# A hybrid decoder block on one core: the first norm's row blocks put in another order

## The chip, the cores and the metric

The kernel runs on one core of a Trainium2 chip. The time is device microseconds of one execution, as the median of several runs. A core has a matrix engine (TensorE, PE in the profile, with PEld for its weight loads), a vector engine (VectorE, DVE), an activation engine (ScalarE, ACT), a general engine (GpSimd, POOL) and a queue engine (SyncE, SP). Each works through its own fixed queue of instructions in order; semaphores tie the queues together. TensorE writes to eight banks of PSUM; everything else lies in SBUF, 128 partitions wide. Transfers from memory are issued by SP, ACT or POOL and run on 16 DMA engines.

## The reference

`x` is 512 rows (tokens) of 2048 columns. What the change touches is the start:

```python
def rmsnorm(x, g):
    xf = x.astype(jnp.float32)
    y = xf * lax.rsqrt(jnp.mean(xf * xf, axis=-1, keepdims=True) + EPS)
    return (y * g.astype(jnp.float32)).astype(x.dtype)
...
        h = rmsnorm(x, g_mix[l])
        z = jnp.einsum('bsd,dc->bsc', h, w_in[l])
        cb, cc, cv, q, k, v, f_logit, gate_c, gate_a = jnp.split(z, SPLIT_POINTS, axis=-1)
```

Behind it come a gated short convolution and eight attention heads with a forget bias, an output projection onto the residual, a second norm with a squared-ReLU MLP of 8192 columns, and a last norm. All of it is in float32.

## The kernel before

**Numbers.** A float32 product is made of three fp32r products: each operand is split into a high part `hi` (ScalarE copies it to fp32r, line 100) and a low part `lo` (VectorE subtracts, line 101); then hi·hi, lo·hi and hi·lo are added up in PSUM. `split` (line 99) does this for weights (tiles `th`, `tl`, two buffers each) and for activations.

**Strassen.** The wide projections use Strassen's scheme in Winograd's form on halves: two halves of the tokens (256 each) by two halves of the 2048 inputs (the even and the odd blocks of 128). `Quarters` (line 378) makes the activation side: `H[i, par]` is the normalised, turned `x` for token half i and input parity par. From it come seven tiles, each with a high and a low part: A11 and A12 (the first token half), A22, and the four sums S1 to S4, which `Quarters.sums` (line 423) makes in place in H with four VectorE steps and then splits in the order S4, S2, S3, S1. The tile of S1 lies over H[0,0] and H[1,0], those of S4 and S2 over the loaded rows of `x`.

**Groups.** A `Group` (line 173) is a set of columns of a weight matrix. Its `head` (line 227) loads two quarters of the weights, and makes the products with A11 (bank "a") and A12 (bank "b"); ScalarE copies a (`snap`), VectorE adds b (`plus`), and the result is stored. Its `tail2` (line 282) loads four quarters and makes the products with S1, S3, S2, S4 and A22, in this order, with VectorE subtracting weights before each. The first groups are gV0 (half of the attention values; `mm_rows`, line 150, with tokens as the output's partitions) and four K/Q groups (`mm_cols`, line 128). Their five heads run first (lines 504 to 506), then the four sums are made, then the five tails. So the heads need the first token half alone, and everything from the first tail on needs all 512 tokens.

**The first norm.** `x` is loaded in four row blocks of 128 tokens (lines 439 to 443) on SP's queue, block 0 in quarters, the others in halves; the small parameter rows are loaded by ACT's queue, turned by TensorE (`pv`, line 453) and copied to `cols`, which holds the gains. For each block ScalarE squares four quarters and adds them up (line 376), VectorE adds the four sums (line 370), POOL raises the result to the power -1/2 (line 372), and VectorE makes a diagonal matrix `dg` of the factors (line 406). TensorE multiplies each 128x128 piece of the rows by `dg` (line 410), which turns and scales it at once; four such pieces fill a bank, 6 or 7 by turns, and VectorE evicts the bank in two steps, one for each parity, with the gain (line 415). Blocks 0 and 1 are written before the squares of 2 and 3; blocks 2 and 3 before the first head.

**What sets the order.** The program is traced as written, and a planner orders each engine's instructions before the run: of those it takes to be ready it issues the earliest in the program. The result is a fixed queue for every engine. Loads wait for a free slot of four (`x0` to `x3`), splits for one of two buffers.

## Time and profile before

| what | value |
|---|---|
| median of three runs | 2464.81 us (2460.54 to 2464.90) |
| the profiled execution's own time | 2467.16 us |
| its span, first to last instruction | 2464.4 us |
| mean granted TensorE clock | 0.998 |
| PE busy | 2435.7 us (99%) |
| DVE busy | 1922.2 us (78%) |
| ACT busy | 1148.4 us (47%) |
| POOL busy | 180.1 us (7%) |
| moved by DMA | 462.98 MB, 188 GB/s |

A row of the timeline has the start in us from the first instruction, the length in us, the engine, the line of the kernel, the operation, the tiles written and read, the shapes, how many instructions were merged, and in square brackets the idle time of the engine before it with what ended it. A row of the chain of waits has the start, the length, the engine, the tile and the line. A row of a group ends with busy us, mean ns of one, and idle time before. Matmuls overlap, so two starts tell more of their price than a length does. An engine that is full on average may be far from full in a stage, and the other way round.

### The profile page before, as it was taken

Reading aid. Unit: us, or ns where it says so; the run is one execution under the profiler, and the core shown is the slowest. Engines: PE = TensorE matmul, PEld = TensorE weight load, DVE = VectorE, ACT = ScalarE, POOL = GpSimd, SP = SyncE. Lnnn points to the kernel's source line nnn. Section 1 sums busy time; section 2 is a strip of 40 time slices with the busy share of each in tenths; the row PEclk is TensorE's granted clock in tenths of the full one; section 3 lists DMA queues with packets and bytes.
Section 4 is the critical chain, followed back from the end, with each engine's and each line's share of the span. In section 5 each row is a group of like instructions: output and inputs, shape, how many; then the busy total and the mean of one; then the engine's idle time right before and its main releaser. Section 6 shows DMA issues by size and latency. Waiting matters only on the chain.

```text
span 2464.4 us, 39238 instructions
## 1 busy us (share of the span) xinstructions
PE 2435.7 (99%) x16910; PEld 2251.2 (91%) x16910; DVE 1922.2 (78%) x1595; ACT 1148.4 (47%) x1144; POOL 180.1 (7%) x280
## 2 busy tenths in 40 slices
PE   7999999999999999999999999999999999999998
PEld 7999999999999988888899999999998888888886
DVE  7977777788777744526688898888987888889898
ACT  6443434334544532225555666656665333333334
POOL 0100000001000000000000000000011001100000
PEclk9999999999999999999999999999999999999999
DMA  7564544456544554335645646656488576655662
GB/s 245 178 186 150 157 133 144 146 175 210 164 125 140 181 175 154 124 128 196 200 164 199 232 176 210 214 194 234 167 298 296 169 250 225 235 194 183 238 229 95
DMA packets 272033, 462.98 MB, mean 188 GB/s; under 512 B 10268, under 2 KB 172180, under 8 KB 271732
## 3 DMA queue, kind: packets, MB, share of 16 engines
q1 hardware_dynamic: 235136, 303.13, 38.7%
q0 software_dynamic: 35856, 156.25, 16.9%
q8 instruction: 132, 2.16, 0.4%
q10 hardware_dynamic: 868, 1.10, 0.1%
q14 instruction: 41, 0.34, 0.0%
HBM read 368.16 MB, written 92.27 MB: 187 GB/s over the span
## 4 chain that ended last, share of the span: by engine, by line
PE 92%; DVE 5%; DMA 1%; issue 1%; ACT 1%; POOL 0%; SPq 0%; DVEq 0%; POOLq 0%; ACTq 0%
PE a L144 6%; PE a L146 6%; PE a L148 6%; PE d L148 5%; PE d L144 5%; PE d L146 5%; PE a L162 4%; PE a L164 4%; PE a L161 4%; PE c L146 4%; PE c L144 4%; PE c L148 4%; PE d L161 2%; PE d L162 2%; PE d L164 2%; PE b L144 2%
## 5 line engine op out<-in xcount | busy, mean ns | idle before, releaser
L100 ACT ACTIVATE th<-x 128x2048 fp32r<-128x2048 f32 (+1 forms) x252 | 483.1, 1917 | 497.3 <-DVE x L104 161.7
L101 DVE TENSOR_TENSOR tl<-x,th 128x2048 fp32r<-128x2048 f32 (+1 forms) x252 | 575.4, 2287 | 169.3 <-ACT th L100 154.6
L104 DVE TENSOR_TENSOR x<-x,x 128x2048 f32<-128x2048 f32 (+1 forms) x144 | 329.4, 2288 | 11.4 <-DMA x<-in_w_in_dram 5.5
L100 ACT ACTIVATE th<-y 128x2048 fp32r<-128x2048 f32 x81 | 155.5, 1921 | 225.4 <-PE a L162 138.5
L101 DVE TENSOR_TENSOR tl<-raw,th 128x2048 fp32r<-128x2048 f32 x40 | 91.7, 2292 | 150.8 <-ACT th L100 150.3
L162 PE MATMUL a<-th,us 128*128 128x512 f32 x512 | 199.2, 389 | 0.0
L161 PE MATMUL a<-th,us 128*128 128x512 f32 x512 | 199.2, 389 | 0.0
L101 DVE TENSOR_TENSOR tl<-y,th 128x2048 fp32r<-128x2048 f32 x81 | 185.1, 2287 | 16.9 <-ACT th L100 16.7
L144 PE MATMUL a<-ST,th 128*128 128x256 f32 x752 | 174.8, 278 | 1.3 <-ACT th L100 1.3
L146 PE MATMUL a<-ST,th 128*128 128x256 f32 x752 | 174.4, 277 | 0.0
L100 ACT ACTIVATE th<-raw 128x2048 fp32r<-128x2048 f32 x40 | 76.7, 1918 | 176.4 <-PE pt L344 62.6
L144 PEld LDWEIGHTS a<-ST,th 128*128 128x128 f32 x752 | 141.4, 188 | 1.7 <-ACT th L100 1.7
L146 PEld LDWEIGHTS a<-ST,th 128*128 128x128 f32 x752 | 141.4, 188 | 0.0
L164 PE MATMUL a<-tl,us 128*128 128x512 f32 x512 | 136.9, 389 | 0.6 <-DVE tl L101 0.6
L144 PE MATMUL c<-S,th 128*128 128x256 f32 x576 | 134.7, 278 | 0.0
L146 PE MATMUL c<-S,th 128*128 128x256 f32 x576 | 134.5, 278 | 0.0
L144 PE MATMUL d<-ST,th 128*128 128x256 f32 x512 | 118.9, 277 | 0.0
L146 PE MATMUL d<-ST,th 128*128 128x256 f32 x512 | 118.9, 277 | 0.0
L100 ACT ACTIVATE th<-t 128x2048 fp32r<-128x2048 f32 x31 | 59.5, 1919 | 125.1 <-DVE t L104 72.7
L164 PEld LDWEIGHTS a<-tl,us 128*128 128x128 f32 x512 | 95.9, 188 | 21.1 <-DVE tl L101 1.0
L161 PEld LDWEIGHTS a<-th,us 128*128 128x128 f32 x512 | 96.1, 188 | 20.0
L162 PEld LDWEIGHTS a<-th,us 128*128 128x128 f32 x512 | 96.1, 188 | 19.9
(296 smaller groups left out, 6381.0 us busy)
## 6 DMA issues: line engine op xcount, KB each, us to landing
x<-in_w_in_dram SPq DMA_DIRECT2D x86, 1024.0 KB, 5.8
x<-in_w_ff_dram SPq DMA_DIRECT2D x64, 1024.0 KB, 7.4
y<-in_w_ff_dram SPq DMA_DIRECT2D x64, 1024.0 KB, 8.0
us<-s_d POOLq DMA_DIRECT2D x48, 1024.0 KB, 9.5
s_d<-rh POOLq DMA_DIRECT2D x32, 896.0 KB, 5.5
s_d<-r POOLq DMA_DIRECT2D x32, 896.0 KB, 5.7
raw<-in_w_mix_out_dram SPq DMA_DIRECT2D x24, 1024.0 KB, 5.1
g_d<-o POOLq DMA_DIRECT2D x32, 256.0 KB, 3.0
```

What stands on the lines that cost most here:

```text
L100: nc.scalar.activation(out=hi, in_=src, func=AF.Copy)
L101: nc.vector.tensor_tensor(out=lo, in0=src, in1=hi.bitcast(F32), op=ALU.subtract)
L104: nc.vector.tensor_tensor(out=out, in0=a, in1=b, op=ALU.subtract)
L144: nc.tensor.matmul(o, hi[:, q, js], Sh, start=first and q == 0 and j == 0, stop=False, skip_group_check=True)
L146: nc.tensor.matmul(o, hi[:, q, js], Sl, start=False, stop=False, skip_group_check=True)
L148: nc.tensor.matmul(o, lo[:, q, js], Sh, start=False, stop=q == nq - 1, skip_group_check=True)
L161: nc.tensor.matmul(o, Sh, hi[:, q, :], start=begin and q == 0, stop=False, skip_group_check=True)
L162: nc.tensor.matmul(o, Sl, hi[:, q, :], start=False, stop=False, skip_group_check=True)
L164: nc.tensor.matmul(o, Sh, lo[:, q, :], start=False, stop=q == nq - 1, skip_group_check=True)
```

## The change

Five things in the opening are different.

- Loads: block 0 and block 1 of `x` are issued by SP and ACT by turns; the parameter rows go to POOL's queue; the weights of gV0's head are issued before the rows of blocks 2 and 3, which come as one transfer each.
- 28 turns of the identity into an unused bank are put in front of the first block's turn.
- Block 0 is turned into four banks (0, 1, 2, 5) and block 1 into 6, 7, 0, 1, with the eviction on VectorE written as a function of its own (`gained`). Block 1 and the later ones have one square over 2048 columns; POOL adds epsilon and takes the power, and ScalarE makes the diagonal.
- gV0's head (`first_rows`) runs its product with A11 for the first 128 tokens, then for the second; block 1's eviction and the splits of A12 stand between.
- Blocks 2 and 3 are squared after gV0's head (the square of block 2 writes the cell that gV0's copy reads as its scale, 1.0), turned together in pieces of two, eight pieces after the head of the first K/Q group and eight after that of the second, and evicted by ScalarE with the gain as its scale (`gained_both`). A22 is then split in one.

```diff
--- before.py
+++ after.py
@@ -399,26 +399,35 @@
         def put(self, n, src, ts=slice(0, HS)):
             split(src[:, :, ts], self.ST[n][:, 0, :, ts], self.ST[n][:, 1, :, ts])
 
-        def block(self, xt, part, t):
-            r = rstd_of(part)
+        def turn(self, ts, cs, dgs, banks):
+
+            n = S // (P * len(ts))
+            out = []
+            for c, i in zip(range(cs.start, cs.stop, n), banks):
+                pt = bank(i, "ptr").rearrange("p (k s) -> p k s", k=n)
+                for k in range(n):
+                    for e, t in enumerate(ts):
+                        nc.tensor.matmul(pt[:, k, e * P:(e + 1) * P], xin[t][:, (c + k) * P:(c + k + 1) * P], dgs[t],
+                                         start=True, stop=True)
+                out.append((c, pt))
+            return out
+
+        def gained(self, t, turned):
+
             i, ts = t // 2, slice(t % 2 * P, (t % 2 + 1) * P)
-            dg = const.tile([P, P], F32, tag="dg", name="dg", bufs=2)
-            nc.vector.tensor_scalar(out=dg, in0=ident, scalar1=r, scalar2=None, op0=ALU.mult)
-            for c in range(4):
-                pt = bank(6 + c % 2, "ptr")
-                for k in range(4):
-                    nc.tensor.matmul(pt[:, k * P:(k + 1) * P], xt[:, (4 * c + k) * P:(4 * c + k + 1) * P], dg,
-                                     start=True, stop=True)
-                p2 = pt.rearrange("p (q two b) -> p two q b", two=2, b=P)
-                g2 = self.gT[:, 4 * c:4 * c + 4].rearrange("p (q two) -> p two q", two=2)
+            for c, pt in turned:
+                p2 = pt.rearrange("p (q two) b -> p two q b", two=2)
+                g2 = self.gT[:, c:c + 4].rearrange("p (q two) -> p two q", two=2)
                 for par in range(2):
-                    nc.vector.tensor_tensor(out=self.H[i, par][:, 2 * c:2 * c + 2, ts], in0=p2[:, par],
+                    nc.vector.tensor_tensor(out=self.H[i, par][:, c // 2:c // 2 + 2, ts], in0=p2[:, par],
                                             in1=g2[:, par].unsqueeze(2).to_broadcast([P, 2, P]), op=ALU.mult)
-            if i == 0:
-                self.put("A11", self.H[0, 0], ts)
-                self.put("A12", self.H[0, 1], ts)
-            else:
-                self.put("A22", self.H[1, 1], ts)
+
+        def gained_both(self, i, turned):
+
+            for c, pt in turned:
+                for k in range(2):
+                    nc.scalar.activation(out=self.H[i, k][:, c // 2, :], in_=pt[:, k, :], func=AF.Copy,
+                                         scale=self.gT[:, c + k:c + k + 1])
 
         def sums(self):
             H = self.H
@@ -433,43 +442,65 @@
 
     ph = ExitStack()
     px = ph.enter_context(phase("px"))
-    xin = []
     xp = [pair(2 + i, F32, "xn") for i in range(2)]
-    for t in range(NT):
-        h = xp[t // 2][:, t % 2]
-        n = 4 if t == 0 else 2
+    xin = [xp[t // 2][:, t % 2] for t in range(NT)]
+
+    def load_rows(t, n, queues):
+        w = D // n
         for i in range(n):
-            nc.sync.dma_start(out=h[:, i * D // n:(i + 1) * D // n], in_=x[t * P:(t + 1) * P, i * D // n:(i + 1) * D // n])
-        xin.append(h)
-        if t == 0:
-            rows = main.tile([NV, P], F32, tag="x3", name="rows")
-            r0 = 0
-            for src, n in ((g_mix[0], KT), (g_mlp[0], KT), (b_gate[0], 2 * KT)):
-                nc.scalar.dma_start(out=rows[r0:r0 + n, :], in_=src.rearrange("(k p) -> k p", p=P))
-                r0 += n
-            nc.scalar.dma_start(out=rows[r0:r0 + 3 * CT, :], in_=conv_w[0].rearrange("j (k p) -> (j k) p", p=P))
-            nc.scalar.dma_start(out=bf, in_=b_f.to_broadcast([P, NH]))
-            pv = bank(7, "pv")
-            nc.tensor.transpose(pv[:, :NV], rows, ident[:NV, :NV])
-            nc.vector.tensor_copy(cols, pv[:, :NV])
+            queues[i % len(queues)].dma_start(out=xin[t][:, i * w:(i + 1) * w], in_=x[t * P:(t + 1) * P, i * w:(i + 1) * w])
+
+    load_rows(0, 4, (nc.sync, nc.scalar))
+    load_rows(1, 2, (nc.sync, nc.scalar))
+    rows = main.tile([NV, P], F32, tag="x3", name="rows")
+    r0 = 0
+    for src, n in ((g_mix[0], KT), (g_mlp[0], KT), (b_gate[0], 2 * KT)):
+        nc.gpsimd.dma_start(out=rows[r0:r0 + n, :], in_=src.rearrange("(k p) -> k p", p=P))
+        r0 += n
+    nc.gpsimd.dma_start(out=rows[r0:r0 + 3 * CT, :], in_=conv_w[0].rearrange("j (k p) -> (j k) p", p=P))
+    nc.gpsimd.dma_start(out=bf, in_=b_f.to_broadcast([P, NH]))
+
+    spare = bank(3, "spare")
+    for i in range(28):
+        nc.tensor.transpose(spare[:, :P], ident, ident)
+    pv = bank(7, "pv")
+    nc.tensor.transpose(pv[:, :NV], rows, ident[:NV, :NV])
+    nc.vector.tensor_copy(cols, pv[:, :NV])
     ss1 = const.tile([P, NT, 5], F32, name="ss1")
     nc.vector.memset(ss1[:, :, 4:5], EPS)
     Q1 = Quarters(px, gmixT)
 
-    junk = pair(6, F32, "junk")[:, 1]
-
-    def squares(t):
-        for i in range(4):
-            square_part(xin[t][:, i * S:(i + 1) * S], ss1[:, t, i:i + 1], junk[:, i * S:(i + 1) * S])
-
-    for t in (0, 1):
-        squares(t)
-        Q1.block(xin[t], ss1[:, t, :], t)
-    for t in (2, 3):
-        squares(t)
-    Q1.tiles("A22")
-    for t in (2, 3):
-        Q1.block(xin[t], ss1[:, t, :], t)
+    both = pair(6, F32, "junk")
+    dg2, junk = both[:, 0], both[:, 1]
+
+    dgs = {t: main.tile([P, WBUF], F32, tag="th", name="dg", bufs=2)[:, :P] for t in range(2)}
+    dgs.update((t, dg2[:, t % 2 * P:(t % 2 + 1) * P]) for t in (2, 3))
+
+    def squares(t, n):
+
+        w = D // n
+        for i in range(n):
+            square_part(xin[t][:, i * w:(i + 1) * w], ss1[:, t, i:i + 1], junk[:, i * w:(i + 1) * w])
+
+    def factors_of(ts):
+
+        n = len(ts)
+        v, r = (stat.tile([P, 2], F32, tag=f"{k}2", name=k) for k in "vr")
+        t = slice(ts[0], ts[0] + n)
+        nc.gpsimd.tensor_tensor(out=v[:, :n], in0=ss1[:, t, 0], in1=ss1[:, t, 4], op=ALU.add)
+        nc.gpsimd.tensor_tensor(out=r[:, :n], in0=v[:, :n], in1=mhalf.to_broadcast([P, n]), op=ALU.pow)
+        for k, t in enumerate(ts):
+            nc.scalar.activation(out=dgs[t], in_=ident, func=AF.Copy, scale=r[:, k:k + 1])
+
+
+    nc.vector.memset(ss1[:, 2:4, 0:1], 1.0)
+    squares(0, 4)
+    nc.vector.tensor_scalar(out=dgs[0], in0=ident, scalar1=rstd_of(ss1[:, 0, :]), scalar2=None, op0=ALU.mult)
+    Q1.gained(0, Q1.turn((0,), range(0, KT), dgs, (0, 1, 2, 5)))
+    Q1.put("A11", Q1.H[0, 0], slice(0, P))
+    squares(1, 1)
+    factors_of((1,))
+    second_block = Q1.turn((1,), range(0, KT), dgs, (6, 7, 0, 1))
 
 
     def store_v(c0, w):
@@ -501,9 +532,42 @@
         g.head(True)
         g.tail2()
 
+    def first_rows():
+
+        g = gV0
+        X = {(0, 0): g.load(0, 0), (1, 0): g.load(1, 0)}
+        load_rows(2, 1, (nc.sync,))
+        load_rows(3, 1, (nc.sync,))
+        g.a = g.acc("a")
+        hi, lo = parts([P, KT // 2, g.w])
+        split(X[0, 0], hi, lo)
+        mm_rows(g.a, g.ST("A11"), hi, lo, True, (0,))
+        Q1.put("A12", Q1.H[0, 1], slice(0, P))
+        Q1.gained(1, second_block)
+        Q1.put("A11", Q1.H[0, 0], slice(P, HS))
+        mm_rows(g.a, g.ST("A11"), hi, lo, True, (1,))
+        s1 = g.snap(g.a, ss1[:, 2, 0:1])
+        Q1.put("A12", Q1.H[0, 1], slice(P, HS))
+        b = g.acc("b")
+        g.run(b, "A12", X[1, 0], True)
+        g.plus(s1, b)
+        g.done(0, 0)
+        g.done(1, 0)
+        g.put(0, 0, s1)
+
     heads = [gV0] + [kq(hp, ((a,), (3,), (6,), (7,))) for hp, a in enumerate((0, 1, 2, 5))]
-    for g in heads:
+    first_rows()
+    for t in (2, 3):
+        squares(t, 1)
+    factors_of((2, 3))
+    Q1.tiles("A22")
+    for k, g in enumerate(heads[1:]):
         g.head()
+        if k < 2:
+            for c in range(8 * k, 8 * k + 8, 2):
+                Q1.gained_both(1, Q1.turn((2, 3), range(c, c + 2), dgs, (6 + c // 2 % 2,)))
+        if k == 1:
+            Q1.put("A22", Q1.H[1, 1])
     Q1.sums()
     ph.close()
     for g in heads:
@@ -852,7 +916,7 @@
         ms = const.tile([P, NT], F32, name="ms")
         nc.vector.tensor_reduce(out=ms, in_=ss2, axis=AX.X, op=ALU.add)
         nc.gpsimd.tensor_tensor(out=r, in0=ms, in1=mhalf.to_broadcast([P, NT]), op=ALU.pow)
-        ones = const.tile([P, P], F32, tag="dg", name="ones", bufs=2)
+        ones = const.tile([P, P], F32, name="ones")
         nc.vector.memset(ones, 1.0 / S)
         pt = bank(6, "mean")
         nc.tensor.matmul(pt[:, :NT], ones, ms, start=True, stop=True)
```

## The prediction

> **What bounds the kernel now.** I read the engine shares first, then busy time by stretches of the opening, then TensorE's timeline to the first product on a sum tile, then VectorE's over the same time. These are the engine row and three stretches (after the length: PE, PEld, DVE, ACT and POOL busy, clock, DMA share, GB/s):
> ```profile
> PE 2435.7 (99%) x16910; PEld 2251.2 (91%) x16910; DVE 1922.2 (78%) x1595; ACT 1148.4 (47%) x1144; POOL 180.1 (7%) x280
> 0.00:25.00 25.00, 12.36 (x72) 11.71 (x73) 9.51 (x31) 15.82 (x38) 3.33 (x13) 0.93 0.93 306
> 25.00:86.40 61.40, 61.40 (x539) 61.30 (x539) 60.34 (x50) 34.70 (x24) 6.27 (x8) 1.00 0.65 202
> 86.50:120.00 33.50, 33.50 (x296) 33.50 (x295) 29.13 (x19) 11.67 (x10) 2.90 (x4) 1.00 0.53 157
> ```
> TensorE is the bound, and what can be won lies in the first 25 us, where it stands idle for 12.6 us. But from 25 to 86.4 us VectorE is busy 60.3 of 61.4 us: second engine, as full as the first. Whatever is late for VectorE there has no room to be made up.
>
> TensorE, from the timeline and the chain of waits:
> ```profile
> 6.31 0.38 PE L453 MATMUL pv<-ident,rows 88*128 88x88 f32 x1 [6.31 <-DMA rows<-in_conv_w_dram]
> 8.63 3.78 PE L410 MATMUL ptr<-dg,xn 128*128 128x128 f32 x16 [1.94 <-DVE dg L406]
> 14.59 6.48 PE L410 MATMUL ptr<-dg,xn 128*128 128x128 f32 x40 [2.17 <-issue]
> 23.29 2.02 PE L410 MATMUL ptr<-dg,xn 128*128 128x128 f32 x16 [2.22 <-DVE h L415]
> 25.06 0.36 PE L161 MATMUL a<-th,A 128*128 128x256 f32 x1
> 29.62 1.78 PE ptr L410 x16
> 42.88 0.28 PE L144 MATMUL a<-A,th 128*128 128x256 f32 x1
> 46.68 1.81 PE a L148 x16
> 52.12 1.81 PE b L148 x16
> 86.41 0.28 PE L161 MATMUL c<-th,S 128*128 128x256 f32 x1
> ```
> A float32 turn has two records, 32 a row block, so four blocks are 128 records: 0.111 us each warm (1.78/16), 0.236 in the first piece (3.78/16). One Strassen product of 48 matmuls takes 5.44 us (52.12 - 46.68). At 42.88 us the four turns and both head products of the first group (gV0) are done and the four K/Q heads begin; at 86.41 comes the first product on a sum tile, S1. It needs the four sums of the halves, and those need all four row blocks.
>
> VectorE's side of that:
> ```profile
> 8.50 0.21 DVE L543 CAST identb<-ident 128x128 bf16<-128x128 f32 x1
> 13.65 0.16 DVE L370 TENSOR_REDUCE v<-ss 128x1 f32<-128x5 f32 x1 [4.78 <-ACT junk L376]
> 13.73 0.76 DVE L415 TENSOR_TENSOR h<-ptr,cols 128x256 f32<-128x256 f32 x2
> 39.07 0.76 DVE L415 TENSOR_TENSOR h<-ptr,cols 128x256 f32<-128x256 f32 x2 [1.04 <-PE ptr L410]
> 41.94 1.22 DVE L101 TENSOR_TENSOR A<-h,A 128x1024 fp32r<-128x1024 f32 x1
> 43.68 2.28 DVE L107 TENSOR_TENSOR h<-h,h 128x2048 f32<-128x2048 f32 x1
> 45.88 2.29 DVE L101 TENSOR_TENSOR tl<-x,th 128x2048 fp32r<-128x2048 f32 x1
> 73.50 2.28 DVE L101 TENSOR_TENSOR S<-h,S 128x2048 fp32r<-128x2048 f32 x1
> 75.77 2.29 DVE L104 TENSOR_TENSOR x<-x,x 128x2048 f32<-128x2048 f32 x1
> 43.08 0.69 DVE L107 TENSOR_TENSOR o<-b,o 128x512 f32<-128x512 f32 x1
> ```
> The last row block is evicted at 39.8; from the first sum (43.68) to the end of S1's low part (75.77) VectorE runs eight such steps, four sums and four low parts, mixed with six weight splits and two 0.6 us additions: 14 x 2.2 + 1.2 = 32.0 us without a gap. That is 36 us from the last eviction to S1, and S1 is used 10.6 us after it is ready. Line 543 at 8.50 us, ninety lines ahead of its place, shows that the planner fills idle engines with whatever is ready, in program order among the ready.
>
> **The change, part by part.**
>
> *Loads.* SP's ten x loads take its queue until 8.5 us, and the first weight is issued only then:
> ```profile
> 0.81 7.73 SPq L442 DMA_DIRECT2D xn<-in_x_dram  x10
> 8.58 11.82 SPq L188 DMA_DIRECT2D x<-in_w_in_dram  x4
> 4.42 0.63 ACT L376 ACTIVATE junk<-xn 128x512 f32<-128x512 f32 x1 [1.66 <-DMA xn<-in_x_dram]
> 9.47 0.63 ACT L376 ACTIVATE junk<-xn 128x512 f32<-128x512 f32 x1 [2.12 <-DMA xn<-in_x_dram]
> 12.29 0.63 ACT L376 ACTIVATE junk<-xn 128x512 f32<-128x512 f32 x1 [1.49 <-DMA xn<-in_x_dram]
> 10.00:15.00 5.00, 2.83 (x16) 2.56 (x15) 1.35 (x5) 3.52 (x13) 0.55 (x1) 1.00 1.00 372
> 7.69 0.55 POOL L372 TENSOR_TENSOR r<-v,mhalf 128x1 f32<-128x1 f32 x1 [6.17 <-DVE v L370]
> 55.68 0.73 POOL L486 DMA_DIRECT2D kq_d<-o  x1 [10.73 <-DVE o L107]
> ```
> Afterwards blocks 0 and 1 (2 MB) are issued on two queues at once. With the first 0.26 MB in by 4.4 us and the 0.37 MB per us of 10 to 15 us, block 0 is in by about 6.5 (as now), block 1 by 9.3 instead of 12.3, gV0's two weights by 12 and 15, blocks 2 and 3 by 18 and 21, then the next weights by 24 and 27. The parameter rows go to POOL: five issues at 0.73 us end near 5.2 us, ahead of the power that POOL computes at 7.7, so nothing queues behind them; landing at 8.5 they put TensorE's `pv` turn and the first block at 8.9. Cost 0.3 us; bounds 0 and 2.
>
> *Idle turns.* 28 turns of the identity at 0.111 to 0.236 us are 3.1 to 6.6 us, from about 1.6 us: they end before 8.3 and cost nothing. What they may bring is the first block at 0.111 instead of 0.236, up to 4.0 us over 32 records. The clock row:
> ```profile
> 15.00:20.00 5.00, 5.00 (x32) 4.98 (x30) 2.96 (x10) 4.67 (x11) 0.55 (x1) 0.66 1.08 361
> ```
> Here TensorE had stood idle for 2.17 us (12.4 to 14.6), and 3.4 us of the stretch then ran at half rate ((1 - 0.66) x 5 / 0.5). Between idle turns and block 0 lie up to 3 us, so the warmth may be gone again; I take it as kept and hold 4.0 us for the range. By the row, an idle time as long as the 9 us found below can bring the same 3.4 us at half rate, 1.7 us of loss. The Trainium skill, "TensorE: Matmul & The Clock Gate", Part 1, says that half rate is the state after an idle window of about 3.4 us, and that a busy one lifts it; this trace shows the drop after less idle time. By that rule too the products behind that wait start at half rate.
>
> *Blocks 0 and 1.* Block 0: factor at 8.6, turn 8.9 to 12.5 into four banks, evicted bank by bank by 13.4. Now its first eviction stands in VectorE's queue behind the reduction at 13.65 that waits for block 1; that wait goes. Block 1: one square of 2.0 us (an estimate: four quarters at 0.63 without three of their reads) to 11.4, two POOL steps at 0.55, a ScalarE diagonal of 0.3 (estimate, half the width of the 0.474 eviction below), with the handovers 13.0; turn to 16.6. What is late next is VectorE: low parts of the weights (2.2) and of A11's first half (1.14), so the first products run from 18.4; then block 1's eviction (four pairs of 0.76 that overlap a little, 2.8) and A11's other half, so the second 128 tokens of A11 wait to 25.5. TensorE: 7.1 us turns, 11.3 us products, 3.5 us idle from 8.9 on: the K/Q heads begin at 30.9. Now they begin at 42.88 with 7.1 us of turns more behind them. **Gain at this point: 42.9 - 30.9 - 7.1 = 4.9 us.**
>
> *Blocks 2 and 3 behind the first products.* Their squares wait for gV0's copy (it reads the scale 1.0 from the cell that the square overwrites), so the diagonals are ready at 34.2, while the head of K/Q group 0 is running; the turns stand in the program after that head and after the next:
>
> 30.9 + 10.9 + 3.55 + 10.9 + 3.55 = 59.8; with short waits for the two banks the last turn ends at 60.2, and ScalarE has evicted it at 61.3 (39.8 now). ScalarE's price:
> ```profile
> L777 ACT ACTIVATE up<-ptr,cols x16: 453/474/499, 1098.1 to 1229.1; 128x256 f32<-128x256 f32 x16
> 50.40 1.93 ACT L100 ACTIVATE S<-h 128x2048 fp32r<-128x2048 f32 x1 [1.28 <-DVE h L104]
> ```
> Sixteen at 0.474 us fit beside the products, since ScalarE is free 26.7 of 61.4 us. VectorE sheds 16 evictions (5.5 us), two reductions and three diagonals: about 6.5 us, but early, where it now stands idle: between 27 and 63 us it has only weight splits to do, since sums cannot start.
>
> *What is late next.* From 61.3: ScalarE's high part of A22, 1.9. Then VectorE from 63.2: low part of A22, four sums, four low parts (9 x 2.2 = 19.8), between them the two weight splits of the last head (4.4), two additions (1.2) and the subtraction that makes S1's weights (2.2): 27.6, so S1's low part is done at 90.8. TensorE has two heads left at 60, 21.8 us, and is through at 81.7. **Wait: 9.1 us.** S1's place in the order can't move forward: its tile lies over the halves that S2 and S3 are made from. Behind it the queue stays late: the weights of S3 and S2 are subtracted by VectorE after S1's split, and TensorE waits 1.1 us before each; after S2 the stock is rebuilt. **2.2 us.** S1 thus starts at 90.8 instead of 86.4.
>
> *The rest* (bank and tile names, `ones` with a tile of its own) is the same work in the same place: 0.
>
> **Sum.** -4.9 + 9.1 + 2.2 = +6.4 us. The same laying of rows end to end puts S1 of the kernel before at 84.2, where the trace has 86.4: fixed queue orders meet data at other times than planned. I add 1.5 us for that and the half clock together: **+8**. The profiled execution was 2467.16 us with a span of 2464.40, 2.35 above the median of 2464.81; the difference goes on the median: **2473 us**.
>
> **Rivals.**
>
> 1. *Faster.* The planner, which takes what is ready, turns blocks 2 and 3 one head earlier, because it believes K/Q weights to be late. The wait is gone if the last eviction comes by 81.7 - 29.5 = 52 us instead of 61.3: that is, if the second eight turns stand before the head of K/Q group 1 (49 us). For it: turns and products do mix at 25 us now. Against: the diagonals come at 34, when the weights of both next heads have landed. Then -4.9 stays: 2460. Chance 0.17.
> 2. *Nothing to measure.* The planner gives the sums precedence over splits and the subtraction (up to 6.6 us), the heads' splits still being in time. Wait 3 to 6, no later ones: 2463 to 2469, say 2466. Against: in the rows at 43.68 and 45.88 a split comes between two sums. Chance 0.18.
> 3. *Slower still.* Half clock in block 0 and late rows take the opening's gain: 4.0 + 1.7, all of it shifting the sums too: 2478. Chance 0.15.
> 4. The forecast, 2469 to 2477: chance 0.50.
>
> **How the numbers follow.** From 2461 to 2480 lies all but the lower half of the first rival and the end of the third, about 0.15. This kernel's runs can tell no less than 0.2%, 4.9 us: faster than 2459.9 is the first rival with a little given to the band (0.17), the band holds the second and the rims of its neighbours (0.18), the rest is slower (0.65).
>
> **What would show it.** Right: the K/Q heads begin near 31 us, the last turn ends near 60, the first sum on VectorE comes after 63, and TensorE has an idle time of 6 to 12 us before the first product on S1, released by VectorE's low part of S1 or ScalarE's weights. The idle share of the first 25 us falls by less than 5 us. Wrong: if the turns of blocks 2 and 3 are done by 52 us, or if the first product on S1 stands before 86.4 us.

## The result, and the profile after

| | before | after |
|---|---|---|
| median, seven runs each on one chip | 2464.81 us | 2473.74 us (2469.53 to 2479.20) |
| profiled execution | 2467.16 us | 2475.31 us |
| its span | 2464.4 us | 2473.5 us |
| ratio of the medians, 95% interval | | 1.0033 [1.0018, 1.0048] |

The change makes the kernel 0.33% slower, 8.9 us; 2473 us was forecast. The engine row of the page after:

```profile
PE 2440.2 (99%) x16938; PEld 2253.9 (91%) x16938; DVE 1917.3 (78%) x1573; ACT 1153.7 (47%) x1144; POOL 185.3 (7%) x286
```

On average nothing has changed. The stretches of the opening (length; PE, PEld, DVE, ACT and POOL busy; granted clock; DMA share; GB/s) show what has:

```profile
0.00:25.00 25.00, 18.64 (x126) 18.23 (x127) 12.63 (x30) 13.62 (x19) 5.16 (x17) 0.93 0.96 334
25.00:43.00 18.00, 18.00 (x156) 17.86 (x155) 10.80 (x7) 12.56 (x13) 1.90 (x3) 1.00 0.80 239
43.00:60.00 17.00, 17.00 (x151) 16.89 (x150) 6.56 (x5) 9.24 (x14) 1.14 (x2) 1.00 0.67 216
60.00:80.00 20.00, 20.00 (x177) 19.89 (x176) 15.50 (x9) 10.98 (x12) 1.06 (x2) 1.00 0.47 144
80.00:95.00 15.00, 7.05 (x53) 6.16 (x52) 15.00 (x8) 9.96 (x6) 0.72 (x1) 0.92 0.23 75
95.00:120.00 25.00, 23.28 (x182) 23.08 (x183) 22.16 (x15) 7.20 (x7) 6.13 (x5) 0.91 0.49 139
```

From 25 to 86 us VectorE was full in the kernel before. Now it is busy for 10.8 of 18 us and 6.6 of 17 us while TensorE is full; then, from 80 to 95 us, VectorE is full and TensorE works for 7.05 of 15 us. VectorE was idle early, and TensorE waits for it late. The same in TensorE's timeline:

```profile
2.56 5.54 PE L465 MATMUL spare<-ident 128*128 128x128 f32 x28 [2.56 <-POOL ident masks.py:199]
9.91 0.27 PE L467 MATMUL pv<-ident,rows 88*128 88x88 f32 x1 [1.81 <-DMA rows<-in_conv_w_dram]
10.03 9.01 PE L410 MATMUL ptr<-dg,xn 128*128 128x128 f32 x64
...
32.80 0.29 PE L144 MATMUL a<-A,th 128*128 128x256 f32 x1
...
82.08 1.98 PE L148 MATMUL b<-A,tl 128*128 128x256 f32 x16
84.30 0.38 PE L161 MATMUL d<-th,S 128*128 128x256 f32 x1 [0.25 <-ACT th L100]
86.65 0.38 PE L162 MATMUL d<-th,S 128*128 128x256 f32 x1 [1.97 <-DVE S L101]
...
87.11 0.28 PE L161 MATMUL d<-th,S 128*128 128x256 f32 x1
...
88.41 0.28 PE L162 MATMUL d<-th,S 128*128 128x256 f32 x1
93.60 0.58 PE L161 MATMUL c<-th,S 128*128 128x256 f32 x1 [4.91 <-ACT S L100]
96.06 0.58 PE L162 MATMUL c<-th,S 128*128 128x256 f32 x1 [1.88 <-DVE S L101]
```

The K/Q heads begin at 32.80 (42.88 before) and end at 83.8; the first product on a sum tile begins at 84.30, and the one on S1 gets its low part at 96.06. Between them TensorE starts sixteen matmuls of S3's product. Counted from start to start, less the usual step, the pauses from 83.8 to 96.4 add up to 10.4 us, and another of 0.95 us comes at 108.7: **11.4 us of waiting**. In the kernel before TensorE went from the last head straight into S1 at 86.41.

VectorE's timeline over the same time, and ScalarE's at its two ends:

```profile
31.32 2.29 DVE L101 TENSOR_TENSOR tl<-x,th 128x2048 fp32r<-128x2048 f32 x1 [3.00 <-ACT th L100]
...
53.25 2.29 DVE L101 TENSOR_TENSOR tl<-x,th 128x2048 fp32r<-128x2048 f32 x1 [6.39 <-ACT th L100]
...
65.24 2.29 DVE L101 TENSOR_TENSOR A<-h,A 128x2048 fp32r<-128x2048 f32 x1 [3.73 <-ACT A L100]
68.30 2.29 DVE L104 TENSOR_TENSOR x<-x,x 128x2048 f32<-128x2048 f32 x1 [0.76 <-DMA x<-in_w_in_dram]
...
72.71 2.28 DVE L107 TENSOR_TENSOR h<-h,h 128x2048 f32<-128x2048 f32 x1
...
79.91 2.29 DVE L104 TENSOR_TENSOR x<-x,x 128x2048 f32<-128x2048 f32 x1
...
89.32 6.69 DVE L101 TENSOR_TENSOR S<-h,S 128x2048 fp32r<-128x2048 f32 x3
```

```profile
9.85 1.91 ACT L376 ACTIVATE junk<-xn 128x2048 f32<-128x2048 f32 x1 [2.03 <-DMA xn<-in_x_dram]
...
31.90 1.92 ACT L376 ACTIVATE junk<-xn 128x2048 f32<-128x2048 f32 x1
...
39.32 0.67 ACT L493 ACTIVATE junk<-ident,r 128x128 f32<-128x128 f32 x2
...
61.52 1.73 ACT L429 ACTIVATE h<-ptr,cols 128x256 f32<-128x256 f32 x4 [0.35 <-PE ptr L410]
63.29 1.92 ACT L100 ACTIVATE A<-h 128x2048 fp32r<-128x2048 f32 x1
```

The last eviction ends at 63.3 (39.8 before). Only then can VectorE split A22 (65.24) and make the first sum (72.71); S1's low part, the last of the three at 89.32, ends at 96.01 (75.79 before). From 65.24 on VectorE has no pause but one of 0.76 us. Before that, from 25 us on, it had pauses of 3.00, 6.39, 3.73 us and more, 22.1 us in all.

### The profile page after: what moved, and what is told of

The parts are those of the page before. It is cut to its first block, busy times and chain, and to the rows that moved or that the text cites. A ratio compares the mean times of both kernels' runs of the same rounds, so it can differ in the third digit from the quotient of the medians.

```text
span 2473.5 us, 39270 instructions
## 1 busy us (share of the span) xinstructions
PE 2440.2 (99%) x16938; PEld 2253.9 (91%) x16938; DVE 1917.3 (78%) x1573; ACT 1153.7 (47%) x1144; POOL 185.3 (7%) x286
## 4 chain that ended last, share of the span: by engine, by line
PE 88%; DVE 6%; DMA 2%; issue 2%; ACT 1%; POOL 0%; SPq 0%; DVEq 0%; POOLq 0%; ACTq 0%
PE a L144 6%; PE a L146 6%; PE a L148 5%; PE d L144 4%; PE d L146 4%; PE d L148 4%; PE a L164 4%; PE a L162 4%; PE a L161 4%; PE c L146 4%; PE c L144 4%; PE c L148 3%; DVE tl L101 2%; PE pn L351 2%; PE pn L352 2%; PE pt L344 2%
```

## The experiments

The theory: S1 comes when VectorE has done a fixed amount of work, and what delays it is the time that VectorE stands idle before the sums may start. The rivals: the wait goes with the last eviction at a constant distance (the prediction's 29.5 us); it is the evictions' engine; or the opening, clock and loads make the difference. All edits are against the changed kernel. The table has, from each profiled execution, in us: the first K/Q head, the last eviction, the end of S1's low part, VectorE's idle time from 25 us to then, and the first product of the tail of K/Q group 0, which shows what the opening cost TensorE up to there. "Busy" is S1's time less 25 and less the idle time, so the three add up by construction, and the theory is tested by whether "busy" stays the same. The ratio is to the kernel before on the same chip. The kernel before took 2465.5 to 2468.8 us on the chips of the experiments (2464.8 on that of the result), so ratios can be compared and medians cannot. Expected times in us go by the 2464.8.

| kernel | K/Q heads | last eviction | S1 low | VectorE idle | busy | K/Q 0's tail | median | ratio |
|---|---|---|---|---|---|---|---|---|
| before | 42.88 | 39.82 | 75.79 | 1.04 | 49.8 | 113.61 | 2464.81 | 1 |
| after | 32.80 | 63.26 | 96.01 | 22.14 | 48.9 | 124.85 | 2473.74 | 1.0033 |
| one head later | 31.99 | 73.75 | 98.56 | 24.28 | 49.3 | 126.31 | 2476.83 | 1.0030 |
| one head sooner | 32.02 | 52.46 | 86.68 | 17.81 | 43.9 | 119.26 | 2466.69 | 0.9991 |
| all turns at once | 32.35 | 48.72 | 85.75 | 16.64 | 44.1 | 117.20 | 2465.97 | 0.9991 |
| two low parts out | 32.77 | 63.65 | 92.10 | 22.68 | 44.4 | 121.31 | 2472.56 | 1.0024 |
| VectorE evicts | 30.96 | 63.91 | 95.81 | 17.23 | 53.6 | 126.39 | 2476.49 | 1.0044 |
| warm wait | 31.03 | 61.91 | 95.02 | 22.93 | 47.1 | 123.86 | 2472.63 | 1.0023 |
| opening undone | 35.24 | 66.13 | 98.10 | 22.41 | 50.7 | 127.04 | 2476.00 | 1.0036 |
| idle turns bridged (one run) | 32.32 | 63.19 | 95.44 | 22.08 | 48.4 | 124.41 | 2477.45 | |
| no idle turns (one run) | 34.53 | 65.41 | 97.30 | 23.03 | 49.3 | 126.15 | 2472.31 | |
| no hold | 40.02 | 48.05 | 87.27 | 12.31 | 50.0 | 119.97 | 2470.63 | 1.0017 |
| shorter hold | 33.95 | 41.50 | 80.73 | 11.86 | 43.9 | 113.45 | 2461.04 | 0.9975 |
| shorter hold, bridged | 33.92 | 41.52 | 80.75 | 10.83 | 44.9 | 113.47 | 2463.19 | 0.9987 |

### Where the turns of blocks 2 and 3 stand

One edit in three settings. The two sets of eight turns, which the change puts behind the heads of K/Q groups 0 and 1, stand one head later (behind those of groups 1 and 2, the setting in the diff), one head sooner (in front of those of groups 0 and 1: `{0: (0,), 1: (1,)}`), or both in front of the first K/Q head (`{0: (0, 1)}`).

```diff
+    def turn_half(h):
+        for c in range(8 * h, 8 * h + 8, 2):
+            Q1.gained_both(1, Q1.turn((2, 3), range(c, c + 2), dgs, (6 + c // 2 % 2,)))
+        if h == 1:
+            Q1.put("A22", Q1.H[1, 1])
     for k, g in enumerate(heads[1:]):
+        for h in {2: (0,), 3: (1,)}.get(k, ()):
+            turn_half(h)
         g.head()
-        if k < 2:
...
```

> The two sets stand one head later each, before the third and before the fourth K/Q head. Theory: one head and its additions to it later, 14.5 us, but less of the heads' own splits is left between the sums (one split, 2.2 us, and one addition fewer): the wait grows by 11 to 14.5 us, 2485 to 2488 us. Rival (VectorE's total work sets S1's time, not the turns): unchanged, 2474.

> The two sets of eight turns stand one head earlier each, before the first and before the second K/Q head. Theory: last eviction near 49 to 50 us, which is just inside the 52 us where the wait ends: no wait or up to 1 us, 2461 to 2464 us, as when all sixteen come at once. Rival (every us of delay of the turns costs, without a threshold): in the middle between all at once and the changed kernel.

> All sixteen turns of blocks 2 and 3 stand before the first K/Q head; all else as changed. Theory (the loss is the wait for the sums, 29.5 us from the last eviction to S1): last eviction near 50 us, S1's low part near 80, before the heads end at about 83, so no wait; the opening's 3 us stay: 2461 to 2463 us. Rival (the wait is TensorE's half clock or POOL's and the weights' lateness at that place, whatever the turns do): 2470 to 2474.

Measured: later 2476.83 us, 1.0030 [1.0017, 1.0043]; sooner 2466.69, 0.9991 [0.9980, 1.0001]; at once 2465.97, 0.9991 [0.9979, 1.0002]. The two earlier settings take the change's loss back, and a gain beyond that is not shown. Their ratios lie in the ranges that the theory gave (2461 to 2464 us is 0.9985 to 0.9997), but not for its reason: S1's low part came at 85.7 and 86.7 instead of near 80, and at K/Q 0's tail TensorE is still 3.6 and 5.6 us behind the kernel before. The later setting was a clear miss of the theory, and its rival (unchanged) came nearer, with 1.0030 against 1.0033: the last eviction came 10.5 us later than in the changed kernel and S1 only 2.6 us. VectorE's timeline of the kernel with the turns one head later shows why:

```profile
62.53 2.29 DVE L104 TENSOR_TENSOR x<-x,x 128x2048 f32<-128x2048 f32 x1 [5.61 <-DMA x<-in_w_in_dram]
64.74 2.29 DVE L101 TENSOR_TENSOR tl<-x,th 128x2048 fp32r<-128x2048 f32 x1
...
72.43 2.29 DVE L104 TENSOR_TENSOR x<-x,x 128x2048 f32<-128x2048 f32 x1
75.73 2.29 DVE L101 TENSOR_TENSOR A<-h,A 128x2048 fp32r<-128x2048 f32 x1 [1.01 <-ACT A L100]
...
91.87 6.69 DVE L101 TENSOR_TENSOR S<-h,S 128x2048 fp32r<-128x2048 f32 x3
```

The two subtractions of tail weights (62.53, 72.43) and splits that stood between the sums in the changed kernel were done here before A22. From last eviction to S1 it is 24.8 us, against 32.8 in the changed kernel, 37.0 with the turns at once and 36.0 before. So a constant distance is refuted. VectorE's busy time is 49 us in both; idle time grew by 2.1 us and S1 by 2.6. A fixed amount of work is not the whole story either: with the turns earlier "busy" is 44 us, because other work of VectorE was placed behind S1.

With all turns at once the idle time falls by only 5.5 us, because the diagonals still come late: A22's split follows a pause of 9.41 us. From then on VectorE is full and TensorE loses time in small pieces. A row of the timeline and a stretch of that kernel:

```profile
50.70 2.29 DVE L101 TENSOR_TENSOR A<-h,A 128x2048 fp32r<-128x2048 f32 x1 [9.41 <-ACT A L100]
```

```profile
60.00:85.00 25.00, 24.47 (x216) 24.27 (x215) 24.97 (x14) 15.67 (x10) 1.45 (x2) 1.00 0.64 195
```

### What VectorE has to do

*Two low parts out.* A22's and S4's low parts are zeros written by POOL, so their products with the high part of the weights lack a term and the output is less exact; the matmuls stay.

```diff
         def put(self, n, src, ts=slice(0, HS)):
+            if n in ("A22", "S4"):
+                nc.scalar.activation(out=self.ST[n][:, 0, :, ts], in_=src[:, :, ts], func=AF.Copy)
+                nc.gpsimd.memset(self.ST[n].bitcast(F32)[:, 1, :, ts], 0.0)
+                return
             split(...)
```

> The low parts of A22 and S4 are not computed; POOL writes zeros there, so that two steps of 2.2 us are off VectorE between the last eviction and S1 (the result is less exact). All else as changed. Theory (VectorE, busy without a gap from the last eviction on, sets when S1 is ready): S1's products 4.4 us sooner, the wait 4.4 us shorter, 2468.5 to 2470 us. Rival (ScalarE's high parts, or the weights of the first tail, set it): unchanged, 2473 to 2474.

Measured: 2472.56 us, 1.0024 [1.0011, 1.0037]. VectorE's busy time falls by 4.5 us, S1 comes 3.9 us sooner and K/Q 0's tail 3.5 us sooner, with the last eviction where it was (63.65). The mechanism is there, in a size a little under the 4.4 us of work taken away; the gain in the total, 0.9 parts in a thousand (2.2 us), is smaller still and within what the intervals leave open.

*VectorE evicts.* The other direction: sixteen evictions are put back on VectorE.

```diff
-                    nc.scalar.activation(out=self.H[i, k][:, c // 2, :], in_=pt[:, k, :], func=AF.Copy,
-                                         scale=self.gT[:, c + k:c + k + 1])
+                    nc.vector.tensor_scalar(out=self.H[i, k][:, c // 2, :], in0=pt[:, k, :],
+                                            scalar1=self.gT[:, c + k:c + k + 1], scalar2=None, op0=ALU.mult)
```

> Blocks 2 and 3 are evicted by VectorE (sixteen steps with the gain as a scalar) instead of ScalarE; all else as changed. Theory (VectorE stands idle 22 us before the sums, so it takes the evictions in idle time): last eviction near 63 us, S1's low part at 95.5 to 97, 2473 to 2474.5 us, ratio 1.003 to 1.004. Rival (VectorE's work counts in full): 5.6 us (sixteen by 0.35) later, ratio 1.0055.

Measured: 2476.49 us, 1.0044 [1.0032, 1.0056]. VectorE's timeline, and TensorE's:

```profile
44.93 1.65 DVE L429 TENSOR_SCALAR h<-ptr,cols 128x256 f32<-128x256 f32 x4
...
62.14 1.77 DVE L429 TENSOR_SCALAR h<-ptr,cols 128x256 f32<-128x256 f32 x4 [0.53 <-PE ptr L410]
```

```profile
80.66 1.98 PE L148 MATMUL b<-A,tl 128*128 128x256 f32 x16
93.40 0.58 PE L161 MATMUL c<-th,S 128*128 128x256 f32 x1 [10.77 <-ACT S L100]
95.86 0.58 PE L162 MATMUL c<-th,S 128*128 128x256 f32 x1 [1.88 <-DVE S L101]
```

S1's low part is ready at 95.81, against 96.01: 4.7 us more of work on VectorE went into 4.9 us less of idle time, as the theory had it. Handing the evictions to ScalarE, a part of the change, buys nothing where they stand. The time is above the theory's range all the same. Two differences are to be seen: here S1's product stands first in TensorE's queue, so nothing of S3's runs in the wait (11.0 us in one piece from the end of the heads); and the granted clock from 85 to 95 us is 0.62, against 0.88 in the changed kernel. Up to K/Q 0's tail that is 1.5 us more, though the K/Q heads began 1.8 us sooner. The intervals of the two ratios overlap, so that the total differs is not shown.

### The opening

*Opening undone* takes back the loads, the idle turns, the place of the first weights and the first group by 128 tokens, and keeps blocks 2 and 3 late.

```diff
-    load_rows(0, 4, (nc.sync, nc.scalar))
-    load_rows(1, 2, (nc.sync, nc.scalar))
+    load_rows(0, 4, (nc.sync,))
...
+    for t in (1, 2, 3):
+        load_rows(t, 2, (nc.sync,))
...
-        mm_rows(g.a, g.ST("A11"), hi, lo, True, (0,))
...
+        g.run(g.a, "A11", X[0, 0], True)
```

> The late part of the change stays (blocks 2 and 3 behind the products, evicted by ScalarE); the loads, the idle turns, the order of the first weights and the first group by 128 tokens are as before. Theory (the opening gains 3 us and the lateness costs 11 to 13, and they add up): the K/Q heads begin at 35.5 to 37 us, S1's products at 97 to 100, and the time is 2476 to 2478 us, ratio 1.0045 to 1.0055. Rival (the late part's cost shrinks by what the opening loses, since VectorE's idle time is what counts): ratio 1.003 to 1.004.

Measured: 2476.00 us, 1.0036 [1.0023, 1.0049]. The K/Q heads begin 2.4 us later than after the change, the last eviction comes 2.9 us later and S1 2.1 us later. So between these two executions the opening's parts bring 2.4 us where they act and 2.1 us at S1; in the total they are lost in the spread (1.0036 against 1.0033). The late part alone is enough for the whole loss. The traces are near the theory's places (heads at 35.24 against 35.5 to 37, S1 at 98.1 against 97 to 100), the ratio lies in the rival's range; which of the two holds is not shown.

*No idle turns* leaves out the 28 turns; *idle turns bridged* (the diff) has 40, and moves the turn of the parameter rows behind block 0's, so that TensorE hardly pauses.

```diff
-    for i in range(28):
+    for i in range(40):
...
+    first_block = Q1.turn((0,), range(0, KT), dgs, (0, 1, 2, 5))
     pv = bank(7, "pv")
...
-    Q1.gained(0, Q1.turn((0,), range(0, KT), dgs, (0, 1, 2, 5)))
+    Q1.gained(0, first_block)
```

> The 28 idle turns are left out; all else as changed. Theory (their warmth was lost in the gap before block 0, so they bought little): the K/Q heads begin at 32.8 to 33.8 us. Rival (they save up to 4.0 us on the first block): 35 to 37.

> 40 idle turns instead of 28, and the turn of the parameter rows behind the first block's turn instead of ahead of it; all else as changed. In the changed kernel the first block began at 10.0 us, behind a wait of 1.8 us for the rows, and 3.4 us of it ran at half rate. Theory: the block begins near 9.1 us at full rate, and the K/Q heads begin at 30.3 to 31 us instead of 32.8. Rival (VectorE's evictions and splits set the opening from there on): 32 to 32.8.

One run of each, 2472.31 and 2477.45 us, from which no verdict on the time is drawn. In the traces the K/Q heads begin at 34.53 without idle turns; with them they begin between 31.0 and 32.8 in the seven kernels of the table from "after" to "warm wait", which have the change's opening, so the idle turns bring 1.7 us or more, by this one trace without them. With the bridge it is 32.32, inside that range, though block 0's turn runs at full clock. TensorE's timeline of the bridged kernel, and a stretch:

```profile
13.27 3.84 PE L410 MATMUL ptr<-dg,xn 128*128 128x128 f32 x32
17.03 0.38 PE L161 MATMUL a<-th,A 128*128 128x256 f32 x1
19.61 0.58 PE L162 MATMUL a<-th,A 128*128 128x256 f32 x1 [2.19 <-DVE A L101]
```

```profile
19.00:23.00 4.00, 3.39 (x17) 3.40 (x18) 4.00 (x10) 0.72 (x1) 0.00 (x0) 0.57 1.04 350
```

The turns of both blocks are done by 17.0 (18.8 after the change), and then TensorE waits 2.19 us for VectorE's low part of A11. The turns no longer set the first products; the splits do. Nor did the bridge do away with the half clock: behind this wait it is at half rate for 3.4 us, (1 - 0.57) x 4 / 0.5, now over the first products instead of block 0's turn. The traces with the turns one head later, one head sooner and all at once have such a stretch too, between 19.7 and 23.6 us, and their heads begin at 32.0 to 32.4; the two without any in the opening, VectorE evicts and warm wait, begin at 31.0.

### The wait itself

*Warm wait* takes the four sums out of `Quarters.sums` and makes them in front of a set of 56 turns of the finished sum H[0,1] into a free bank, which TensorE does in the wait.

```diff
+    keep = bank(3, "keep")
+    H = Q1.H
+    add(H[1, 1], H[1, 0], H[1, 1])
+    sub(H[1, 0], H[0, 0], H[1, 0])
+    sub(H[0, 0], H[1, 1], H[0, 0])
+    sub(H[0, 1], H[0, 1], H[0, 0])
+    for i in range(56):
+        nc.tensor.transpose(keep[:, :P], H[0, 1][:, i % 8, :P], ident)
     Q1.sums()
```

> 56 turns of a finished sum into an unused bank fill TensorE's wait before S1, so that its clock stays up; nothing else is moved. If the half clock behind the wait is a loss of its own: the 1.6 us of S1's first 16 matmuls come back, 2472 us, and the granted clock stays 1.0 there. If VectorE's and ScalarE's lateness sets the next products anyway: TensorE waits as much longer before S2's products, 2473 to 2474.

Measured: 2472.63 us, 1.0023 [1.0010, 1.0035], an interval that overlaps that of the changed kernel. The clock is at half rate for 3.4 us inside the wait and back at full rate before S1's products. In the changed kernel the half clock behind the wait stretched fourteen steps between matmuls from 0.113 to 0.213 us, 1.4 us in all. TensorE's rows behind S1, the first of the changed kernel, the other two of this one:

```profile
109.67 1.21 PE L164 MATMUL a<-tl,S 128*128 128x256 f32 x8 [0.66 <-DVE tl L101]
```

```profile
105.45 0.39 PE L161 MATMUL a<-th,S 128*128 128x256 f32 x1 [0.37 <-ACT th L100]
108.68 1.21 PE L164 MATMUL a<-tl,S 128*128 128x256 f32 x8 [1.08 <-DVE tl L101]
```

The 1.4 us came back as waiting: from the end of S1's low part to K/Q 0's tail it is 28.84 us in both kernels. The tail comes 1.0 us sooner because S1 does (95.02 instead of 96.01), in a trace whose K/Q heads began 1.8 us sooner. So the second case that was written down came about: the half clock is real, but taking it away gains nothing, because VectorE's and ScalarE's lateness sets the next products.

### What makes the diagonals late

After the change the squares of blocks 2 and 3 are held back until gV0's copy, since they overwrite the cell that the copy reads as its scale. *No hold* has all turns at once and takes this hold away; *shorter hold* has all turns at once and hangs the hold on an earlier step, the high part of A12's second 128 tokens.

```diff
-        s1 = g.snap(g.a, ss1[:, 2, 0:1])
-        Q1.put("A12", Q1.H[0, 1], slice(P, HS))
+        s1 = g.snap(g.a)
+        ts = slice(P, HS)
+        hi, lo = (Q1.ST["A12"][:, e, :, ts] for e in range(2))
+        nc.scalar.activation(out=hi, in_=Q1.H[0, 1][:, :, ts], func=AF.Copy, scale=ss1[:, 2, 0:1])
+        nc.vector.tensor_tensor(out=lo, in0=Q1.H[0, 1][:, :, ts], in1=hi.bitcast(F32), op=ALU.subtract)
```

> As with all turns before the K/Q heads, and the squares of blocks 2 and 3 no longer wait for gV0's copy (its scale is the constant 1 again). Theory (what decides is how long VectorE stands idle before the sums: 1 us in the kernel before, 22 in the changed one, some 17 with all turns at once but held): last eviction near 40 us, VectorE idle 5 to 8 us, S1 ready near 78, no wait before or after it, and the opening's 3 us stay: 2460.5 to 2462.5 on a chip where the kernel before takes 2464.8, a ratio of 0.998 to 0.999. Rival (the squares and evictions in ScalarE's queue delay gV0's head by as much): ratio 1.000.

> All turns of blocks 2 and 3 before the K/Q heads, and their squares held only until A12's second high part (which now reads the scale cell) instead of gV0's copy. Without any hold the square of block 2 stood in ScalarE's queue in front of the first weights' split and TensorE lost 6 us. Theory (VectorE's idle time before the sums decides, and the hold keeps ScalarE's queue clear): the K/Q heads begin at 33 us beside the turns, last eviction at 41 to 43 us, S1 ready at 80 to 82, TensorE at S1 by 84 to 85 without a wait, 1.5 to 2.5 us ahead of the kernel before: ratio 0.999. Rival (in this order ScalarE's and VectorE's queues cost the opening's gain once more): ratio 1.000 to 1.002.

No hold: 2470.63 us, 1.0017 [1.0006, 1.0027], worse than all turns at once with the hold. The theory missed (S1 at 87.27 instead of 78, VectorE idle for 12.3 us instead of 5 to 8), and the time is above the rival's too. ScalarE's timeline and TensorE's in that kernel:

```profile
18.14 1.91 ACT L376 ACTIVATE junk<-xn 128x2048 f32<-128x2048 f32 x1 [4.90 <-DMA xn<-in_x_dram]
```

```profile
22.94 0.58 PE L161 MATMUL a<-th,A 128*128 128x256 f32 x1 [5.73 <-ACT A L100]
```

The square of block 2 comes ahead of the first weights' split in ScalarE's queue and waits there for its rows until 18.14; everything behind it waits too, and TensorE stands idle for 5.7 us. Its clock is then at half rate for 6.8 of the 10 us from 20 to 30 (granted clock 0.66). The hold has a purpose, but it holds too long.

Shorter hold: **2461.04 us, 0.9975 [0.9965, 0.9985]**, faster than both kernels. Its timelines of VectorE and TensorE, and a stretch:

```profile
43.49 2.29 DVE L101 TENSOR_TENSOR A<-h,A 128x2048 fp32r<-128x2048 f32 x1 [7.61 <-ACT A L100]
...
78.44 2.28 DVE L101 TENSOR_TENSOR S<-h,S 128x2048 fp32r<-128x2048 f32 x1
```

```profile
83.32 0.28 PE L161 MATMUL c<-th,S 128*128 128x256 f32 x1
...
85.02 0.28 PE L162 MATMUL c<-th,S 128*128 128x256 f32 x1
```

```profile
60.00:85.00 25.00, 25.00 (x223) 25.00 (x222) 25.00 (x13) 12.51 (x8) 5.66 (x5) 1.00 0.64 191
```

The last eviction is at 41.5; S1's low part ends at 80.73, ahead of the last head's end (83.3); TensorE and VectorE are both full from 60 to 85 us, and S1's product follows the heads without a pause. Later waits of 0.95, 0.74 and 0.62 us remain. VectorE's idle time is 11.9 us, still eleven more than before, but busy time is 43.9: six us of other work now stand behind S1 instead of in front of it. Idle time alone does not decide: without the hold it is nearly the same (12.3 us), but VectorE does 50.0 us of work ahead of S1, and S1 comes 6.5 us later.

*Shorter hold, bridged* adds the bridge of the idle turns to it.

> As with the shorter hold, and 40 idle turns with the rows' turn behind the first block's. In the changed kernel that alone moved block 0's turn by 2 us, but the K/Q heads by 0.5 only. Theory (from block 1 on VectorE and ScalarE set the opening): 0 to 0.5 us less than with the shorter hold alone, ratio 0.999. Rival (the first block's 2 us come through now): ratio 0.998.

Measured: 2463.19 us, 0.9987 [0.9979, 0.9996]; the first K/Q head and S1 are where they were, to 0.03 us. Nothing is gained.

One thing stays open. The shorter hold's median is 5.5 us below the kernel before, but its trace is level with that of the kernel before at K/Q 0's tail (113.45 against 113.61). Its span is 2.3 us shorter (2462.1 against 2464.4), and that comes from behind the opening: steps between matmuls are 0.118 us wide in some stretches and 0.113 in others (see the last section), and behind K/Q 0's tail the wide ones take 9.4 us in its trace and 11.7 in that of the kernel before, counted as what each step of 0.116 to 0.1195 us is longer than 0.1134. Over all fourteen traces it is 3.8 to 14.2 us. One trace of each can't tell whether that belongs to the kernel or to the execution, and the rest of the 5.5 us stands in no trace. So the time is lower, but that it is lower because of the opening is not shown.

## Why the prediction was right, point by point

**Outcome.** Forecast 2473 us with slower at 0.65, measured 2473.74. The case that came is the fourth, the forecast. Between the profiled executions it is 8.15 us, against the +8 of the sum. The mechanism, a wait of TensorE for S1 because VectorE starts the sums late, is the one that was forecast. That the total agrees so closely is luck in part: at K/Q 0's tail, where the forecast's terms end, the loss is 11.2 us, three more than the sum, and the trace gives two of them back behind it for a reason that the sum did not have. One sign failed by its number: TensorE's idle time in the first 25 us fell by 6.3 us (12.6 to 6.4) instead of by less than 5, but 5.5 us of that are the idle turns, which count as busy.

**Opening gain, 4.9 us: the term was too large for this execution.** By its own formula it is 42.88 - 32.80 - 7.1 = 3.0 us. Two steps failed. The parameter rows landed at 9.8 instead of 8.5, so that TensorE waited 1.8 us more and block 0's turn began at 10.03 instead of 8.9; the row at 9.91 names them. And "the warmth kept" failed here: the granted clock was half over 3.4 us of block 0's turn. In two other kernels with the same opening (VectorE evicts, warm wait) it stayed full, and their heads began at 30.96 and 31.03, as forecast (30.9), though the rows landed hardly sooner (TensorE's turn of them at 9.69 and 9.62). So the clock's part is some 1.8 us and differs between traces (1.0 to 1.4 us where the half rate fell on the first products), and the late rows by themselves were made up for before the heads.

**Idle turns at no cost: right**, and worth 1.7 us or more at the heads in the one trace without them.

**Last turn at 60.2, last eviction at 61.3: measured 62.1 and 63.3.** Two us late, as were the heads. The diagonals came at 39.3 instead of 34.2; it didn't matter, since the turns stood behind the head in TensorE's queue until 43.7. It did matter with all turns at once, where VectorE's split of A22 follows a pause of 9.41 us.

**VectorE 27.6 us from A22 to S1: too small.** It took 30.8 (65.24 to 96.01). A second subtraction of tail weights, at 79.91, had been placed between the sums (2.2 us), and a weight came 0.76 us late. S1 thus had its low part at 96.0, not 90.8.

**Wait 9.1 + 2.2 us: measured 10.4 + 0.95.** The sum, 11.4 against 11.3, is right partly by luck: S1 was 5.2 us later than forecast, but TensorE came to it 2.1 us later too, and it filled some of the rest with sixteen matmuls of S3's product, which the prediction had behind S1.

**Queue order and half clock, 1.5 us:** the half clock stretched fourteen steps by 1.4 us in all, and wider steps between matmuls took 0.9. That makes at K/Q 0's tail -2.5 (heads end at 83.9 instead of 86.4) + 11.4 + 1.4 + 0.9 = +11.2, as measured. As a loss of its own the half clock was not borne out: in the warm wait its 1.4 us came back as waiting. The last matmul starts 8.8 us later, and the 2.4 us that the trace gives back behind the tail come from the steps between matmuls: the wide ones take 7.5 us there instead of 11.7, while pauses of over 0.3 us between starts take 1.8 more. What makes steps wide is not known.

**Rival 1, "the wait is gone if the last eviction comes by 52": the threshold was wrong, the price right by luck.** At 52.5 and at 48.7 the total is the band's, and TensorE still loses 5.6 and 3.6 us to K/Q 0's tail against the kernel before. At 41.5 the wait is gone, and the ratio is 0.9975 against the 0.998 that the rival's 2460 makes. But the rival's price was the opening's 4.9 us, and of these 0.2 us are left at K/Q 0's tail. The step that failed is the 29.5 us from eviction to S1: it counted the sums, their splits and the two last heads' work, but with an earlier eviction the splits of all the remaining heads lie in between as well (34.2, 37.0 and 39.2 us at 52.5, 48.7 and 41.5).

**Rival 2** (sums ahead of splits) didn't come; the rows at 79.91 and of the splits stand between the sums. **Rival 3** came in part: the opening's gain was 1.9 us below the forecast 4.9, nearly all of it the half clock.

## What to carry to other kernels

When a second engine is full in a stage, count its idle time from the moment where its input is moved, not the busy share over the kernel: here VectorE stood idle for 22.1 us before the sums, and TensorE waited for 11.4 us from 84 us on; in the shorter hold 11.9 us of idle time left pauses of 2.3 us. It is not one for one, since the order of the other work in VectorE's queue counts too. Moving work behind other work helps only as far as its consumers still have room; take the latest time at which the consumer may start, including all that will be queued in front of it by then. And a wait that holds an instruction back in an in-order queue may be protecting the instructions behind it: shorten it before removing it.

## What the runs showed of the hardware

*The same queue, another clock.* Stretches from 10 to 15 us, the first of the changed kernel, the second of the one in which VectorE evicts; the opening is the same in both.

```profile
10.00:15.00 5.00, 5.00 (x31) 5.00 (x32) 2.15 (x7) 2.25 (x3) 1.09 (x4) 0.66 1.10 366
```

```profile
10.00:15.00 5.00, 5.00 (x46) 5.00 (x46) 3.72 (x11) 3.37 (x4) 1.09 (x4) 1.00 1.09 370
```

TensorE had stood idle for 1.81 us ahead of the turn of the parameter rows in the first and for 2.49 us in the second, and it was the shorter pause that was followed by 3.4 us at half rate, (1 - 0.66) x 5 / 0.5. The Trainium skill, "TensorE: Matmul & The Clock Gate", Part 1, says that the window in which activity is counted runs freely and does not start with the kernel; these two rows agree with it, and with its note that the loss differs between runs. Its idle time of about 3.4 us before the drop is more than the 1.81 us seen here.

*Matmul steps at full clock.* In the changed kernel 256-wide matmuls follow each other by 0.118 us from 87.11 to 88.41 (eleven steps), and in the shorter hold the same form (lines 161 and 162) by 0.113 us from 83.32 to 85.02 (fifteen steps), both at a granted clock of 1.00. Stretches of the wider step lie at other places in each trace: 112 to 148 us before, 92 to 152 after. The shorter hold with and without the bridge are level to 0.02 us at 113.45 and then go on with the one step and the other. It is 4%, some two us in a stretch of 50, and over a whole trace the wide steps add 3.8 to 14.2 us behind K/Q 0's tail, as much as the whole change; no run here shows what causes it.

*A copy that waits for POOL.* VectorE's timeline of the changed kernel, behind S1:

```profile
101.49 0.68 DVE L627 COPY sel<-identb 8x1024 bf16<-8x1024 bf16 x1 [1.08 <-POOL sel L625]
102.10 2.27 DVE L104 TENSOR_TENSOR x<-x,x 128x2048 f32<-128x2048 f32 x1
```

VectorE, for which TensorE waits 0.66 us at 109.67, stands idle for 1.08 us because a small copy waits for POOL ahead of a subtraction of tail weights: work that an order fills in where it takes an engine to be idle can hold up that engine. How much sooner the subtraction could have begun without the copy is not shown.
